# A gate product ahead of v's products, and its weights rounded behind its evacuation, in a two-layer GLA and differential-attention kernel

## The chip, the cores and the metric

One core of a Trainium2 chip runs the whole program. The metric is the device time of one execution in microseconds, the median of several runs. All arithmetic is in fp32 accuracy: TensorE multiplies rounded fp32 values ("high" parts) and adds products with the rounding rest ("low" parts), so nearly every matrix exists as a pair, made by a copy on ScalarE (ACT) and a subtraction on VectorE (DVE).

## The reference, cut to what matters

Sixteen learned rows are put ahead of 512 input rows (528 rows of 1024). Layer one is gated linear attention with four heads, layer two differential attention with eight. What the change touches is the beginning of layer one:

```python
proj = xn @ w_in                       # q, k, v, z and g_lr, of the normalised rows xn
q, k, v, z, g_lr = jnp.split(proj, ...)
lg = jax.nn.log_sigmoid(g_lr @ w_gate_up + b_gate) / GLA_TAU
b = jnp.cumsum(lg, axis=2)             # the decay within a chunk
```

`g_lr` has only 16 columns (the gate product below), `w_gate_up` turns them into 1024 (the decay products). Everything else of a head needs the sums `b`; where they fall too low the program takes another, slower path (the branch below).

## The kernel before, in words

The order of the work. PE's instructions run in the order in which the program issues them. On ACT and DVE a scheduler chooses the order when the program is built, by dependences and priorities (`urgent` raises one), except within a stretch called `ordered` (from L686 to `ordered.close()`, L993), whose ACT and DVE instructions keep the program's order among themselves. `issue_after(i)` puts what a block issues on i's engine behind i. `behind_gate()` (L316) does that with the two instructions in `W.gated`, one of ACT and one of DVE.

Filling. A `Weaver` W holds a queue of generators, each a projection that yields after some matmuls the time that they should take. `W.fill(us)` issues steps of the queue until their times add up to at least `us`. `W.defer(us, f)` calls f once so much has been filled in since. So the program's straight code (the gate product, the decays, the branch) is interleaved on PE with products of v, q, k and z by the numbers in these calls.

Plain products. v (two of its column blocks of 256), q and k of head 0 are made by `plain_unit`: a block of 128 columns takes 8 steps of 0.66, each 6 matmuls of 264 columns, into two PSUM banks; 8 such blocks (4 of v, 2 of q, 2 of k) are 64 steps. The banks alternate (`pb_pair`): `bv`, `by` for v's first block, then two banks `bx` for the second. The gate product's results `pgs` (L955) stand in two `bx` banks, the ones that v's second block takes next. A finished v block is copied out on ACT (L892, behind the gate), and 2.4 us of filled steps later four transposes and one short one turn it to token order (L833, L834, into PSUM tiles `ps`, of which there are four). z's products follow the plain ones; they use sums of token halves (`token_sums(0)` to `token_sums(5)`), whose splits are again one ACT and one DVE instruction of 128x1056.

The gate product (L959 to L983). For each of 8 blocks k of the input width, four matmuls at L967 add to `pgs`; after each but the first stands one step of v's products:

```python
        if k >= 1:                                   # L969
            W.fill(0.6)
...
        if k == 5:                                   # L975
...
            wur = T(gp, [P, D], F32R, "z")           # L981
            act.activation(wur, wup, AF.Copy)
            dve.tensor_tensor(wur[64:96], wup[64:96], wur[64:96].bitcast(F32), op=ALU.subtract)
```

`wur` is the rounded `w_gate_up`, in 128x1024, with rows 64 to 95 turned into the low part (L982 on ACT, L983 on DVE).

Its evacuation (L984 to L992). For each of the two banks: an ACT copy (L987), two DVE copies (L988, L989), an ACT copy (L990) and a DVE subtraction (L991), into `gs` and `gh`. The last ACT and DVE instructions of these become `W.gated`.

The decays (L1015 to L1028). After `W.fill(4.0)`, `decay(k)` for k = 0 to 7: two matmuls of `wur` with `gs` into two `ps` tiles (L1006), three functions on ACT (L1007 to L1009), a DVE subtraction that frees the tiles (L1012) and a running sum on DVE into `b_all` (L1013); then `W.fill(3.5)` (2.0 after the first). After k = 1 to 4 comes `token_sums(k - 1)`, with `behind_gate()` from k = 3.

The branch (L1034 to L1264). DVE reduces `b_all` to a flag `fl` (L1034, L1035). After `W.fill(2.4)` a product of one element brings the flag to partition 0 (L1258), DVE turns it into an integer `fi` (L1259), PE fills in 4.0 more, and every engine reads `fi` and branches. In these inputs the other path is not taken.

Of the kernel before, what the change touches and what calls it, by code (L numbers as in the profile page):

```python
# [11 lines left out]
F32 = mybir.dt.float32  # L12
F32R = mybir.dt.float32r
I32 = mybir.dt.int32
U16 = mybir.dt.uint16
AF = mybir.ActivationFunctionType
ALU = mybir.AluOpType
# [3 lines left out]
P = 128  # L21
D = 1024
# [186 lines left out]
def trunk(ctx, tc, x, meta, g_norm, gla_w_in, gla_w_gate_up, gla_b_gate, gla_gnorm, gla_w_out,  # L209
# [3 lines left out]
    act, dve, pe, pool, sp = nc.scalar, nc.vector, nc.tensor, nc.gpsimd, nc.sync  # L213
# [17 lines left out]
    def T(p, shape, dt, tag, **kw):  # L231
        uid[0] += 1
        return p.tile(shape, dt, tag=tag, name=f"{tag}_{uid[0]}", **kw)
# [10 lines left out]
    def ps_tile():  # L244
        return T(ps_pool, [P, 512], F32, "ps")
# [43 lines left out]
    W = Weaver()  # L289
# [26 lines left out]
    def behind_gate():  # L316
        st = ExitStack()
        for i in W.gated:
            st.enter_context(tc.issue_after(i.ins))
        return st  # L320
# [211 lines left out]
    gp = gctx.enter_context(tc.tile_pool(name="gp", bufs=1))  # L532
# [62 lines left out]
    def warm_up(n, t=None):  # L595
        t = warm if t is None else t
        for _ in range(n):
            pe.matmul(t[:, :P], ones, ones, start=True, stop=True)
# [23 lines left out]
    wup = v2[1][:, 0, :]  # L622
# [43 lines left out]
    def raw_turn(b, halves=range(2)):  # L666
        n = BLK[b][1]
        for i in halves:
            pt = ps_tile().rearrange("p (k c) -> p k c", k=4)
            raws.setdefault(b, []).append(pt)  # L670
            for k in range(4):
                pe.transpose(pt[:, k, :n], xt[b][:n, (4 * i + k) * P:(4 * i + k + 1) * P], ident[:n, :n])

    def raw_copy(b, i, eng):
        t0, n = BLK[b]
        o, pt = hT[:, 4 * i:4 * i + 4, t0:t0 + n], raws[b][i][:, :, :n]
        if eng is act:
            act.activation(o, pt, AF.Copy)
        else:
            dve.tensor_copy(o, pt)  # L680
# [79 lines left out]
    def token_sums(n):  # L760

        if n == 0:
            dve.tensor_tensor(x1, x1, x2, op=ALU.subtract)
        elif n == 1:
            split(*X["t1"], x1)
        elif n == 2:
            dve.tensor_tensor(x2, x4, x2, op=ALU.subtract)
            dve.tensor_tensor(x4, x4, x1, op=ALU.add)
        elif n == 3:
            split(*X["t2"], x4, scale=-1.0)  # L770
        elif n == 4:
            dve.tensor_tensor(x3, x4, x3, op=ALU.subtract)
            split(*X["t4"], x3)
        else:
            X["t3"] = x_parts(6)
            split(*X["t3"], x2)
# [182 lines left out]
    for k in range(KT):  # L959
        for n in range(2):  # L960
            for i, x in enumerate((X["b11"], b12) if k < 4 else (X["b21"], X["b22"])):
                if k == 0:
                    warm_up((3, 3, 1, 4)[2 * n + i], idle)
                if (k, 2 * n + i) in turns_of:
                    b, half = turns_of[k, 2 * n + i]
                    raw_turn(b, [half])
                pe.matmul(pgs[i][:112, :HT], glr[:, k, :], x[n][:, k % 4, :],  # L967
                          start=k == 0 and n == 0, stop=k == KT - 1 and n == 1)
        if k >= 1:  # L969
            W.fill(0.6)  # L970
        if k == 1:
            raw_turn(3, [0])
        if k == 4:
            raw_turn(0)
        if k == 5:  # L975
            for b in (3, 4):
                for i in range(2):
                    raw_copy(b, i, act)
            raw_copy(0, 0, dve)
            raw_copy(0, 1, act)  # L980
            wur = T(gp, [P, D], F32R, "z")  # L981
            act.activation(wur, wup, AF.Copy)  # L982
            dve.tensor_tensor(wur[64:96], wup[64:96], wur[64:96].bitcast(F32), op=ALU.subtract)  # L983
    gh = T(gp, [P, L], F32R, "a0")  # L984
    for i, pg in enumerate(pgs):
        cs = slice(i * HT, (i + 1) * HT)
        act.activation(gs[0:RANK, cs], pg[0:RANK, :HT], AF.Copy)  # L987
        dve.tensor_copy(gs[64:64 + RANK, cs], pg[64:64 + RANK, :HT])  # L988
        dve.tensor_copy(gs[96:96 + RANK, cs], pg[96:96 + RANK, :HT])  # L989
        high = act.activation(gh[32:32 + RANK, cs], pg[32:32 + RANK, :HT], AF.Copy)  # L990
        low = dve.tensor_tensor(gs[32:32 + RANK, cs], pg[32:32 + RANK, :HT], gh[32:32 + RANK, cs].bitcast(F32), op=ALU.subtract)  # L991
    W.gated = (high, low)  # L992
    ordered.close()  # L993
    ws.held = 0
# [6 lines left out]
    @urgent  # L1001
    def decay(k):
        e = tmp()
        pus = [ps_tile()[:, :HT] for _ in range(2)]
        for i, pu in enumerate(pus):
            pe.matmul(pu, wur[:, k * P:(k + 1) * P], gs[:, i * HT:(i + 1) * HT], start=True, stop=True)  # L1006
            act.activation(e[:, i * HT:(i + 1) * HT], pu, AF.Abs)  # L1007
        act.activation(e, e, AF.Exp, scale=-1.0)
        act.activation(e, e, AF.Ln, bias=one1)  # L1009
        for i, pu in enumerate(pus):  # L1010
            ei = e[:, i * HT:(i + 1) * HT]
            dve.scalar_tensor_tensor(ei, pu, 0.0, ei, op0=ALU.min, op1=ALU.subtract)  # L1012
        dve.tensor_tensor_scan(b_all[:, k, :], carry, e, 0.0, op0=ALU.mult, op1=ALU.add)  # L1013
# [5 lines left out]
    for k in range(KT):  # L1019
        decay(k)  # L1020
        if k == KT - 1:

            tc.mark_branch_hint_location("steep", "LikelyTaken", engines=[
                mybir.EngineType.PE, mybir.EngineType.DVE, mybir.EngineType.Activation, mybir.EngineType.SP])
        W.fill(3.5 if k else 2.0)
        if 1 <= k <= 4:
            with behind_gate() if k >= 3 else ExitStack():
                token_sums(k - 1)  # L1028

    eL = T(hp, [P, KT, 5], F32, "eL")  # L1030
# [222 lines left out]
        W.fill(2.0)  # L1253
        rows(4, prev)

    W.fill(2.4)
    pf = ps_tile()
    pe.matmul(pf[0:1, 0:1], fl[:, 1:2], one1, start=True, stop=True)  # L1258
    told = urgent(dve.tensor_copy)(fi, pf[0:1, 0:1])  # L1259
# [600 lines left out]
def build(shapes):  # L1860
    import concourse.bacc as bacc

    nc = bacc.Bacc("TRN2", target_bir_lowering=False, num_devices=1, dynamic_dma_scratch_size=512)
    args = [nc.dram_tensor(f"in_{n}_dram", shp, F32, kind="ExternalInput").ap() for n, shp in shapes]
    args.append(nc.dram_tensor("out_0_dram", (1, NR, D), F32, kind="ExternalOutput").ap())
    with tile.TileContext(nc) as tc:
        trunk(tc, *args)
    return nc
# [15 lines left out]
```

## Time and profile before

| | us |
|---|---|
| median of 3 runs (lowest, highest) | 991.65 (991.6, 993.63) |
| the profiled execution | 992.74 |
| its span | 991.0 |
| busy in it: PE, PE's weight loads | 971.3, 916.7 |
| busy in it: DVE, ACT, POOL | 777.4, 616.1, 50.8 |
| mean granted TensorE clock | 0.995 |

A line of a timeline gives the start, the busy time, engine, line of the source, operation, output and inputs, shape and count of like instructions in a row; in brackets the idle time of the engine before it and what ended that. A line of waits gives the total, the number and the longest. A line of windows gives the stretch, its length, then busy time and instructions of PE, PE's weight loads, DVE, ACT and POOL, the granted clock, the DMA engines' share and GB/s.

### The profile page before, as it was taken

Reading aid. Unit: us, or ns where it says so; the run is one execution under the profiler, and the core shown is the slowest. Engines: PE = TensorE matmul, PEld = TensorE weight load, DVE = VectorE, ACT = ScalarE, POOL = GpSimd, SP = SyncE. Lnnn points to the kernel's source line nnn. Section 1 sums busy time; section 2 is a strip of 40 time slices with the busy share of each in tenths; the row PEclk is TensorE's granted clock in tenths of the full one; section 3 lists DMA queues with packets and bytes.
Section 4 is the critical chain, followed back from the end, with each engine's and each line's share of the span. In section 5 each row is a group of like instructions: output and inputs, shape, how many; then the busy total and the mean of one; then the engine's idle time right before and its main releaser. Section 6 shows DMA issues by size and latency. Waiting matters only on the chain. (4 is left out here: it accounts for less than half of the span.)

```text
span 991.0 us, 18184 instructions
## 1 busy us (share of the span) xinstructions
PE 971.3 (98%) x7065; PEld 916.7 (93%) x7065; DVE 777.4 (78%) x1584; ACT 616.1 (62%) x1306; POOL 50.8 (5%) x68
## 2 busy tenths in 40 slices
PE   8899999999999999999999999999999999999997
PEld 8898999999999999999899899898998999988896
DVE  7779886788778788556998895887967869677785
ACT  7575865475646656536567676466765667655583
POOL 1000000000000100000000101001010010000001
PEclk9899999999999999999999999999999999999999
DMA  8313313632363312222232524335353351523212
GB/s 192 82 48 88 89 44 130 139 94 78 108 155 91 86 44 85 87 85 77 82 105 61 133 85 145 86 97 135 85 146 86 84 145 45 181 56 89 86 64 85
DMA packets 150474, 96.27 MB, mean 97 GB/s; under 512 B 33117, under 2 KB 136829, under 8 KB 150384
## 3 DMA queue, kind: packets, MB, share of 16 engines
q1 hardware_dynamic: 147504, 89.61, 33.1%
q10 hardware_dynamic: 2880, 5.46, 1.6%
q8 instruction: 57, 0.93, 0.4%
q14 instruction: 33, 0.27, 0.1%
HBM read 83.64 MB, written 7.57 MB: 92 GB/s over the span
## 5 line engine op out<-in xcount | busy, mean ns | idle before, releaser
L270 DVE TENSOR_TENSOR wl<-raw,wh 128x1024 fp32r<-128x1024 f32 x98 | 119.6, 1222 | 27.1 <-ACT wh L269 20.2
L269 ACT ACTIVATE wh<-raw 128x1024 fp32r<-128x1024 f32 x98 | 103.0, 1053 | 52.9 <-PE by L938 27.0
L402 PE MATMUL bv<-x,wh 128*128 128x264 f32 (+1 forms) x656 | 97.5, 287 | 0.8 <-DVE t L448 0.6
L402 PE MATMUL bx<-x,wh 128*128 128x264 f32 (+1 forms) x640 | 95.4, 286 | 0.3
L402 PEld LDWEIGHTS bv<-x,wh 128*128 128x128 f32 x656 | 86.2, 189 | 2.0 <-DVE t L448 1.3
L402 PEld LDWEIGHTS bx<-x,wh 128*128 128x128 f32 x640 | 84.6, 188 | 1.6 <-ACT u L423 0.5
L392 PE MATMUL bx<-x,wh 128*128 128x512 f32 (+1 forms) x256 | 62.5, 386 | 0.0
L423 ACT ACTIVATE u<-bx 128x264 f32<-128x264 f32 (+1 forms) x120 | 45.4, 379 | 24.6 <-PE bx L402 22.2
L270 DVE TENSOR_TENSOR wl<-sum,wh 128x1024 fp32r<-128x1024 f32 x41 | 50.1, 1221 | 11.8 <-ACT wh L269 10.5
L1618 ACT ACTIVATE p<-p,st 128x528 f32<-128x528 f32 (+3 forms) x64 | 36.4, 569 | 30.9 <-DVE st L1616 30.5
L402 PE MATMUL bv<-x,wl 128*128 128x264 f32 (+1 forms) x328 | 54.9, 284 | 0.0
L1654 POOL TENSOR_TENSOR st<-st,mhalf 128x1 f32<-128x1 f32 x32 | 30.7, 959 | 466.5 <-ACT on L1652 422.4
L402 PE MATMUL bx<-x,wl 128*128 128x264 f32 (+1 forms) x320 | 53.6, 285 | 0.0
L392 PEld LDWEIGHTS bx<-x,wh 128*128 128x128 f32 x256 | 44.5, 188 | 7.9
L269 ACT ACTIVATE wh<-sum 128x1024 fp32r<-128x1024 f32 x41 | 43.3, 1056 | 12.0 <-PE bv L402 4.7
L402 PE MATMUL by<-x,a12h 128*128 128x264 f32 (+1 forms) x320 | 47.0, 286 | 0.2
L269 ACT ACTIVATE a11h<-raw 128x512 fp32r<-128x512 f32 x41 | 25.7, 627 | 33.4 <-DMA raw<-in_diff_w_in_dram 18.0
L402 PE MATMUL bx<-x,a11h 128*128 128x264 f32 (+1 forms) x320 | 46.3, 285 | 0.0
L402 PEld LDWEIGHTS bv<-x,wl 128*128 128x128 f32 x328 | 45.8, 188 | 0.0
L402 PEld LDWEIGHTS bx<-x,wl 128*128 128x128 f32 x320 | 45.0, 188 | 0.4 <-DVE wl L270 0.2
L402 PEld LDWEIGHTS bx<-x,a11h 128*128 128x128 f32 x320 | 42.2, 188 | 0.8
L402 PEld LDWEIGHTS by<-x,a12h 128*128 128x128 f32 x320 | 41.8, 188 | 0.7 <-DVE t L448 0.4
(479 smaller groups left out, 2647.1 us busy)
## 6 DMA issues: line engine op xcount, KB each, us to landing
raw<-in_gla_w_in_dram SPq DMA_DIRECT2D x48, 512.0 KB, 4.2
raw<-in_diff_w_in_dram SPq DMA_DIRECT2D x42, 512.0 KB, 5.5
raw<-in_diff_w_in_dram SPq DMA_DIRECT2D x11, 1024.0 KB, 5.8
raw<-in_gla_w_out_dram SPq DMA_DIRECT2D x8, 1024.0 KB, 5.9
raw<-in_diff_w_out_dram SPq DMA_DIRECT2D x8, 1024.0 KB
vd<-planes ACTq DMA_DIRECT2D x12, 268.0 KB, 3.0
vd<-keep ACTq DMA_DIRECT2D x8, 264.0 KB, 2.3
T<-bdr SPq DMA_DIRECT2D x8, 264.0 KB, 3.4
```

The source lines that it names most:

```text
L269: act.activation(hi, src, AF.Copy)
L270: dve.tensor_tensor(lo, src, hi.bitcast(F32), op=ALU.subtract)
L392: pe.matmul(bank, a[:, k, :], b[k] if n0 is None else b[k][:, n0 + i * nn:n0 + (i + 1) * nn], start=n == 0 and ks[0] == 0, stop=n == len(t ...
L402: pe.matmul(bank[:, :x[q].shape[2]], w[p][:, k * P:(k + 1) * P], x[q][:, k, :], start=first and i == 0, stop=i == len(PASSES) - 1, skip_gr ...
L423: W.moved = act.activation(t, self.bx[:, :self.n], AF.Copy, scale=self.sc)
L1618: act.activation(p[:, :nk], p[:, :nk], AF.Exp, scale=-1.0, bias=st[:, m:m + 1], accum_out=st[:, 2 + m:3 + m])
L1654: pool.tensor_tensor(ms, ms, mhalf[:, :1], op=ALU.pow)
```

## The change

Three edits go together. The steps of v's products inside the gate product's loop end with k = 4, so three of seven are issued behind it. `wur` is rounded behind the evacuation instead of at k = 5, and `W.gated` now holds these two instructions; with it, `token_sums(1)` is put behind the gate as well. And 5.0 instead of 2.4 is filled in ahead of the branch's product, which takes up what the loop no longer issues.

```diff
-        if k >= 1:
+        if 1 <= k <= 4:
             W.fill(0.6)
...
             raw_copy(0, 0, dve)
             raw_copy(0, 1, act)
-            wur = T(gp, [P, D], F32R, "z")
-            act.activation(wur, wup, AF.Copy)
-            dve.tensor_tensor(wur[64:96], wup[64:96], wur[64:96].bitcast(F32), op=ALU.subtract)
     gh = T(gp, [P, L], F32R, "a0")
     for i, pg in enumerate(pgs):
         cs = slice(i * HT, (i + 1) * HT)
...
         high = act.activation(gh[32:32 + RANK, cs], pg[32:32 + RANK, :HT], AF.Copy)
         low = dve.tensor_tensor(gs[32:32 + RANK, cs], pg[32:32 + RANK, :HT], gh[32:32 + RANK, cs].bitcast(F32), op=ALU.subtract)
+    wur = T(gp, [P, D], F32R, "z")
+    high = act.activation(wur, wup, AF.Copy)
+    low = dve.tensor_tensor(wur[64:96], wup[64:96], wur[64:96].bitcast(F32), op=ALU.subtract)
     W.gated = (high, low)
...
         if 1 <= k <= 4:
-            with behind_gate() if k >= 3 else ExitStack():
+            with behind_gate() if k >= 2 else ExitStack():
                 token_sums(k - 1)
...
-    W.fill(2.4)
+    W.fill(5.0)
     pf = ps_tile()
     pe.matmul(pf[0:1, 0:1], fl[:, 1:2], one1, start=True, stop=True)
```

## The prediction, made before the run

> **What bounds the kernel now.** I read the page first, then the list of waits of PE, then PE's timeline from 14 to 130 us, then those of DVE and ACT over the same stretch, then the windows.
>
> ```profile
> span 991.0 us, 18184 instructions
> PEclk9899999999999999999999999999999999999999
> ```
>
> The profiled execution took 992.74 us: the span and 1.74 around it. The median of the three runs shown is 991.65, 1.09 less; I take differences from the trace and subtract them from the median. PE is the bound nearly everywhere, so a change is worth what it takes from PE's idle or slow time. The granted clock is below nine tenths only in the second of the 40 slices (24.8 to 49.6 us), where the change lies.
>
> ```profile
> PE bx L845 <- DVE a L991: 2.8, 2, 1.4
> PE ps L1258 <- DVE fl L1035: 2.0, 1, 2.0
> ```
>
> These are the two longest entries among PE's waits in the whole span (total, times, longest), and the change touches both. PE's timeline around them:
>
> ```profile
> 25.80 0.74 PE L967 MATMUL bx<-x,kd 128*112 128x264 f32 x4
> 27.11 0.65 PE L967 MATMUL bx<-x,kd 128*112 128x264 f32 x4
> 28.33 0.65 PE L967 MATMUL bx<-x,kd 128*112 128x264 f32 x4
> 31.82 0.39 PE L845 MATMUL bx<-x,wh 128*128 128x264 f32 x1 [1.40 <-DVE a L991]
> 33.61 3.67 PE L845 MATMUL bx<-x,wh 128*128 128x264 f32 x15 [1.40 <-DVE a L991]
> 38.83 1.03 PE L833 MATMUL ps<-ident,t 128*128 128x128 f32 x4
> 39.73 1.70 PE L845 MATMUL bx<-x,wh 128*128 128x264 f32 x12
> 41.27 0.41 PE L1006 MATMUL ps<-a,z 128*128 128x264 f32 x2
> 56.90 0.28 PE L845 MATMUL bv<-x,wh 128*128 128x264 f32 x1
> 74.62 0.40 PE L1006 MATMUL ps<-a,z 128*128 128x264 f32 x2
> 76.33 2.08 PE L845 MATMUL bx<-x,wh 128*128 128x264 f32 x16
> 79.22 2.11 PE L845 MATMUL bx<-x,wh 128*128 128x264 f32 x16
> 84.30 0.19 PE L1258 MATMUL ps<-ones,fl 128*1 128x1 f32 x2 [1.99 <-DVE fl L1035]
> ```
>
> From 76.33 to 79.22 lie 24 matmuls: 0.12 us each, 0.73 for a step of six. The three groups at L967 are the gate product's last (k = 5, 6, 7), each followed by a step of v's products. Then v's second block wants the gate product's two PSUM banks, and waits for their evacuation, bank by bank, from 30.42 (31.82 less 1.40) to 33.61.
>
> ```profile
> 30.43:33.61 3.18, 0.39 (x2) 0.19 (x2) 2.51 (x10) 1.63 (x4) 0.00 (x0) 0.89 0.00 0
> 33.61:39.73 6.12, 6.12 (x28) 6.06 (x29) 3.54 (x3) 1.24 (x3) 0.00 (x0) 0.50 0.00 1
> ```
>
> The first row has 0.39 us of PE in 3.18; in the second the granted clock is 0.50. So the wait is paid twice: 23 matmuls from 33.61 to 38.83 took 5.22 us, where 23 x 0.12 = 2.8 would do, and the five transposes until 39.73 lost half of their 0.90. Together 2.9 us.
>
> Why the evacuation is late stands in DVE's and ACT's timelines:
>
> ```profile
> 27.51 1.26 DVE L270 TENSOR_TENSOR x<-y,x 128x1056 fp32r<-128x1056 f32 x1 [1.02 <-ACT x L269]
> 28.78 1.22 DVE L983 TENSOR_TENSOR z<-v,z 32x1024 fp32r<-32x1024 f32 x1
> 30.01 0.43 DVE L988 CAST a<-bx 16x264 fp32r<-16x264 f32 x1
> 31.34 0.43 DVE L991 TENSOR_TENSOR a<-bx,a 16x264 fp32r<-16x264 f32 x1
> 33.13 0.42 DVE L991 TENSOR_TENSOR a<-bx,a 16x264 fp32r<-16x264 f32 x1 [0.45 <-ACT a L990]
> 27.38 1.04 ACT L982 ACTIVATE z<-v 128x1024 fp32r<-128x1024 f32 x1
> 28.90 0.38 ACT L987 ACTIVATE a<-bx 16x264 fp32r<-16x264 f32 x1 [0.47 <-PE bx L967]
> ```
>
> DVE does the subtraction of token sum 1 (`x<-y,x`, 1.26) and that of the gate weights (`z<-v,z`, 1.22), and only then takes up the evacuation, 1.1 us after ACT had begun it. From there a half takes 1.77 us (30.01 to 31.77; 31.77 to 33.55).
>
> **The change, part by part.**
>
> Steps behind the gate product. Two of the three steps lie between the last gate groups, so the group at 28.33 moves to 26.87 and ACT's first copy from 28.90 to 27.44. Token sum 1 is now held behind the gate and the weights' rounding comes after the evacuation, so both rows ahead of 30.01 leave. The first half then ends at 27.44 + 0.45 + 1.77 = 29.65, the second at 31.4. PE still has the moved steps: four steps (24 matmuls, 2.9 us) behind the last gate group, to 30.4 as now. The first bank is free before that, the second is awaited for 0.9 us instead of 2.8. PE runs on at 31.45 instead of 33.61: 2.15 saved. With 0.9 us idle instead of 3.2 I expect the clock to stay at 1.0: 2.9 more. Sum 5.05.
>
> [...]
>
> Rounding of the gate weights. It is one ACT instruction (1.04) and one DVE (1.22), now on the path of the first decay product (L1006). ACT's last copy of the evacuation ends one subtraction (0.43) before 31.4, so the rounding runs 31.0 to 32.0 and the subtraction to 33.3. The first decay product now stands behind 11 steps instead of 14 (four plus seven): three steps into the second block, at 31.45 + 17 x 0.12 = 33.5. Cost 0 by 0.2 us of margin; with one more 1.26 us instruction ahead of it on DVE PE would stand 1.1 us, and v's products behind it. It can't gain. What W.gated holds (the split of v's next weights, v's evacuation, token sums 1 to 3) queues behind these two instead, from 33.3 on DVE; now it starts there behind 33.55, so nobody waits longer. No DMA is moved; the weight loads follow the splits that free their buffers.
>
> Decays three steps earlier. The steps counted: 64 plain ones in all; now 7 + 7 + 4 + 7 x 6 = 60 and four in the fill of 2.4, so the branch product stands exactly behind the 64th. After: 57, and the fill of 5.0 takes the seven left and two small steps of z's first product (6 matmuls, 0.73). So PE comes to L1258 at 82.31 - 5.05 + 0.73 = 78.0, with 0.73 of later work done. Whether `fl` is ready then is DVE's affair:
>
> ```profile
> 33.55:84.24 50.69, 48.24 (x371) 47.48 (x371) 40.30 (x64) 35.59 (x70) 0.00 (x0) 0.94 0.23 63
> 64.33:84.24 19.91, 17.78 (x145) 17.36 (x143) 19.84 (x36) 13.35 (x23) 0.00 (x0) 1.00 0.20 53
> 40.54 0.69 DVE L270 TENSOR_TENSOR v<-ps,v 128x512 fp32r<-128x512 f32 x1 [3.39 <-ACT v L269]
> 45.20 0.77 DVE L1012 SCALAR_TENSOR_TENSOR t<-ps,t 128x264 f32<-128x264 f32 x2 [0.21 <-ACT t L1009]
> 64.33 0.69 DVE L337 TENSOR_TENSOR sum<-raw 128x512 f32<-128x512 f32 x1 [2.58 <-DMA raw<-in_gla_w_in_dram]
> ```
>
> From the evacuation to `fl` DVE is busy for 40.30 us (third number pair of the row) and idle for 10.39. Lower bound: from 33.3 without any idle time, with token sum 1 added, 33.3 + 40.30 + 1.26 = 74.9. Upper bound: the idle time as now but for the 3.39 that the slow clock made, 81.9. The nearest row between them is the last: from 64.33 DVE never rests until `fl`, and it began then because a load landed, 7.43 us after PE ended v's last block (56.90), which had freed the buffers. With PE 5.05 earlier that is 59.3, and 19.9 on gives 79.2; token sum 1 fits into the idle time before. I take 79.2, the branch product at 79.3, a wait of 1.3 instead of 2.0. Gain so far: 84.30 - 79.3 + 0.73 = 5.7.
>
> A small new wait: the four transposes and the second decay now follow the first decay within 3.4 us, and a decay holds its PSUM tiles for 4.7 (41.27 to 45.97). If the second gets these tiles it waits 1.3, if the transposes' nothing. I count 0.5. No gain is possible there. **Forecast: 5.2 us less, 991.65 - 5.2 = 986.4.**
>
> Behind the branch both PE and DVE start from `fl`, so all shifts alike, and the two rows of waits above are by far the longest: I count nothing as given back.
>
> **The rivals.**
>
> 1. DVE follows at once (the decays come three steps earlier, so one of them fits into the idle 2.58 before the load). Then PE never waits at L1258 and the product runs at 78.0: 7.0 less, 984.6. For it: the row at 64.33. Against it: that DVE is full afterwards.
>
> 2. DVE keeps all its other idle time, `fl` at 81.9: gain 84.30 - 82.0 + 0.73 = 3.0, 988.6.
>
> 3. The clock falls all the same, because 0.9 us and a stall at the first decay lie close together. Then 2.9 goes; with `fl` bound as before 991.65 - 5.2 + 2.9 = 989.3.
>
> 4. Slower: PSUM tiles. Decays release their tiles on DVE (L1012), in an order fixed when the program is built.
>
> ```profile
> 33.59 1.26 DVE L767 TENSOR_TENSOR y<-y,y 128x1056 f32<-128x1056 f32 x1
> 34.76 1.22 DVE L270 TENSOR_TENSOR wl<-raw,wh 128x1024 fp32r<-128x1024 f32 x1
> 35.89 1.25 DVE L768 TENSOR_TENSOR y<-y,y 128x1056 f32<-128x1056 f32 x1
> 42.26 1.26 DVE L273 SCALAR_TENSOR_TENSOR x<-y,x 128x1056 fp32r<-128x1056 f32 x1 [0.66 <-ACT x L272]
> ```
>
> If these four and token sum 1 (6.25 us) all stand ahead of the first L1012, it ends at 33.3 + 6.25 + 0.77 = 40.3. The second decay, at 36.9, waits 3.4, the clock halves (2.9), and the third, whose tiles the second holds, waits as long again: 9.7 lost against 5.05 won. PE is at L1258 at 87.7 and the end moves by 87.7 - 84.30 - 0.73 = 2.7, to 994.3. It decides against the change from a first release behind 40. For it: today's DVE order has all four ahead of 45.20. Against it: the decays are issued as urgent, and L1012 at 45.20 waited for ACT, not for these.
>
> **How the numbers follow.** A measurement of this kernel can tell about 0.2% (2 us) from no change. Forecast, 985.4 to 987.6: 0.43; rival 1: 0.15; rival 2: 0.16; rival 3 or a like loss: 0.11, half of it within 0.2%; rival 4 and slower: 0.15. Faster by over 0.2%: 0.79; same: 0.06; slower: 0.15. The range from 983.8 to 991.2 leaves out rival 4 and a little at either end.
>
> **What would show it.** Right: the last group of L967 at 26.9; L988 within 0.5 us of L987; one wait of L845 of about 0.9 and the clock at 1.0 through 40 us; the first L1006 near 33.6 without a wait on `z`; the branch product between 78 and 80. Wrong: another DVE or ACT instruction of 1 us ahead of L988 or of the gate weights' subtraction, a half clock behind 31 us, L1006 waiting for L1012, or the gain present at the branch product and gone by the end.

## The result, and the profile after

The changed kernel takes 986.66 us (median of four runs, 985.8 to 987.15) against 991.62 before (991.48 to 993.63): 5.0 us less, a ratio of 0.9944 with a 95% interval from 0.9927 to 0.9962. In a later comparison (e12 below) it was 985.59 against 990.67, 5.1 less, 0.9953 (0.9939 to 0.9967). The forecast was 986.4.

The page of the changed kernel:

```profile
span 984.8 us, 18186 instructions
PEclk9999999999999999999999999999999999999999
```

The second slice, at 8 before, is at 9. PE's waits from 14 to 130 us (total, times, longest):

```profile
PE bx L845 <- DVE a L988: 0.9, 1, 0.9
PE ps L1006 <- DVE v L270: 0.2, 1, 0.2
PE bx L402 <- DVE ks L822: 0.2, 1, 0.2
```

The 2.8 at the gate product's banks has become 0.9 (L988 is the line that was L991), the 2.0 at the branch product is gone. PE's timeline, with the rows that answer to those of before:

```profile
26.45 1.71 PE L967 MATMUL bx<-x,kd 128*112 128x264 f32 x12
32.09 2.07 PE L845 MATMUL bx<-x,wh 128*128 128x264 f32 x15 [0.91 <-DVE a L988]
34.24 0.41 PE L1006 MATMUL ps<-a,z 128*128 128x264 f32 x2
38.28 0.73 PE L1006 MATMUL ps<-a,z 128*128 128x264 f32 x2 [0.20 <-DVE v L270]
67.95 0.41 PE L1006 MATMUL ps<-a,z 128*128 128x264 f32 x2
77.68 0.89 PE L402 MATMUL by<-x,a11h 128*128 128x264 f32 x6
78.50 0.19 PE L1258 MATMUL ps<-ones,fl 128*1 128x1 f32 x2
```

The last three gate groups follow one another (26.45, twelve matmuls), the fifteen matmuls behind the wait take 2.07 us instead of 3.67, and the branch product is reached behind the six matmuls of z (77.68) without a wait. DVE's timeline:

```profile
28.49 0.43 DVE L985 CAST a<-bx 16x264 fp32r<-16x264 f32 x1 [1.35 <-ACT a L984]
31.61 0.43 DVE L988 TENSOR_TENSOR a<-bx,a 16x264 fp32r<-16x264 f32 x1 [0.18 <-ACT a L987]
32.69 1.22 DVE L991 TENSOR_TENSOR z<-v,z 32x1024 fp32r<-32x1024 f32 x1 [0.66 <-ACT z L990]
56.03 0.78 DVE L1012 SCALAR_TENSOR_TENSOR t<-ps,t 128x264 f32<-128x264 f32 x2 [0.71 <-ACT t L1009]
60.17 0.69 DVE L270 TENSOR_TENSOR a11l<-raw,a11h 128x512 fp32r<-128x512 f32 x1 [1.12 <-ACT a11h L269]
76.82 0.14 DVE L1035 TENSOR_SCALAR fl<-fl 128x1 f32<-128x1 f32 x1
```

DVE is idle when the gate product ends and takes up the evacuation at once; the weights' subtraction (32.69) comes behind it, and `fl` is ready at 76.96, 1.5 us before PE asks for it.

All these times are some 0.77 late, because this execution lost time at its beginning: the clock fell there. The windows of PE (busy time, granted clock, DMA share, GB/s), first of this execution, then of another of the same kernel (e12):

```profile
8.00:12.00 4.00, 3.39 (x15) 0.58 1.13 297
32.00:36.00 4.00, 3.91 (x32) 1.00 0.01 2
```

```profile
8.00:12.00 4.00, 3.48 (x30) 1.00 1.13 295
```

PE's timeline in that execution of e12:

```profile
25.69 1.71 PE L967 MATMUL bx<-x,kd 128*112 128x264 f32 x12
31.32 2.09 PE L845 MATMUL bx<-x,wh 128*128 128x264 f32 x15 [0.91 <-DVE a L988]
33.49 0.40 PE L1006 MATMUL ps<-a,z 128*128 128x264 f32 x2
77.74 0.19 PE L1258 MATMUL ps<-ones,fl 128*1 128x1 f32 x2
```

The second has the clock at 1.00 from 8 to 12 us, as the profile of before has, so its times are the ones to hold against before: PE runs on at 31.32 instead of 33.61, the first decay is at 33.49 instead of 41.27, and the branch product at 77.74 instead of 84.30.

### The profile page after: what moved, and what is told of

It is laid out like the page before. It is cut to its first block, busy times and chain, and to the rows that moved or that the text cites. A ratio compares the mean times of both kernels' runs of the same rounds, so it can differ in the third digit from the quotient of the medians.

```text
span 984.8 us, 18186 instructions
## 1 busy us (share of the span) xinstructions
PE 969.7 (98%) x7065; PEld 915.2 (93%) x7065; DVE 777.3 (79%) x1584; ACT 615.6 (63%) x1306; POOL 50.7 (5%) x68
## 3 DMA queue, kind: packets, MB, share of 16 engines
q1 hardware_dynamic: 147504, 89.61, 33.5%
## 5 line engine op out<-in xcount | busy, mean ns | idle before, releaser
L270 DVE TENSOR_TENSOR wl<-raw,wh 128x1024 fp32r<-128x1024 f32 x98 | 119.6, 1222 | 26.9 <-ACT wh L269 19.9
L270 DVE TENSOR_TENSOR wl<-sum,wh 128x1024 fp32r<-128x1024 f32 x41 | 50.1, 1221 | 11.0 <-ACT wh L269 9.7
```

Source lines behind the costliest of these rows:

```text
L270: dve.tensor_tensor(lo, src, hi.bitcast(F32), op=ALU.subtract)
```

## The experiments

The theory to be tested: DVE's two instructions of 1.2 us made the evacuation late, the moved steps cover what is left of it, the clock is paid beside the wait, and the branch product waited for the decays' place in the order. Each result stands against the kernel before on the same chip, median against median, with the ratio and its 95% interval. The 59 executions of the kernel before in these comparisons, on three chips, ran from 988.83 to 995.05.

**e1, the steps and the fill alone.**

```diff
-        if k >= 1:
+        if 1 <= k <= 4:
             W.fill(0.6)
...
-    W.fill(2.4)
+    W.fill(5.0)
```

> Before with the three steps behind the gate product and the fill of 5.0, but the weights still rounded at k = 5 and token sum 1 not held back. Theory (DVE is what makes the evacuation late): DVE still does token sum 1 and the weights' subtraction until about 30.0, the evacuation ends near 33.5 as before, v's second block still waits about 2.8 us and the clock still falls to 0.5; only the wait of 2.0 at the branch product goes, because it stands behind more work and the decays are three steps earlier. Time 989 to 990. Rival (the moved steps are what covers the evacuation): the wait at L845 falls to about 1 and the clock stays at 1.0; 986.5 to 987.5.

989.63 against 991.79, 0.9980 (0.9969 to 0.9991). PE's rows:

```profile
33.33 2.72 PE L845 MATMUL bx<-x,wh 128*128 128x264 f32 x15 [1.40 <-DVE a L991]
81.07 0.19 PE L1258 MATMUL ps<-ones,fl 128*1 128x1 f32 x2
```

As the theory had it: the last gate group came 1.5 us earlier and nothing came of it, since DVE started the evacuation at 29.73 behind the same two instructions; PE waited the same 2.8 us, and the clock fell again (0.58 from 34 to 37 us, 0.85 from 37 to 40). The gain of 2.2 lies at the branch product, which waits no longer: `fl` is ready at 79.32.

**e2, the rounding and the gate alone.** The edits to `wur`, `W.gated` and `behind_gate` without the two others.

> Before with the weights rounded behind the evacuation and token sum 1 behind the gate, but the steps and the fill of 2.4 as before. Theory: the last gate group stays at 28.3, ACT's first copy at 28.9, DVE's first at 29.3 instead of 30.0; the evacuation ends 0.7 us earlier, near 32.85, and PE, out of steps at 30.4, waits about 2.1 instead of 2.8. Whether the clock then falls is open: if it does, 990.9, if not, about 988 less what the branch product's wait gives back. The wait at the branch product stays near 2. Rival (all of the gain is in DVE's order): 987.

989.89 against 991.79, 0.9974 (0.9964 to 0.9985). PE's waits:

```profile
PE bx L845 <- DVE a L988: 2.1, 2, 1.4
PE ps L1258 <- DVE fl L1035: 2.0, 1, 2.0
```

Both waits as expected. Whether the clock falls was the open point, and the executions differ in it: those with a mean granted clock of 0.999 took 987.78 to 988.67, those with 0.995 to 0.996 990.49 to 991.34. The two halves of the change, e1 and e2, bring 2.2 and 1.9, together 4.1 of the 5.0; whether the rest is theirs together or scatter can't be told from these runs.

**e3, fill alone.**

```diff
-    W.fill(2.4)
+    W.fill(4.6)
...
         token_sums(4)
-    W.fill(4.0)
+    W.fill(2.0)
```

> Before with 4.6 instead of 2.4 filled in ahead of the branch product and 2.0 instead of 4.0 behind it, so the branch stands behind the same work: six small steps (2.2 us of PE) move from behind the branch product to ahead of it. Theory: the wait of 2.0 at L1258 goes almost wholly and nothing takes its place: 989.6, and no change at the gate product. Rival (DVE is the bound there, so the wait moves to the next product that needs DVE): 991.6.

993.42 against 991.79, 1.0015 (1.0004 to 1.0025): slower. The theory falls for this edit by itself. The wait moved one step ahead:

```profile
84.17 1.00 PE L402 MATMUL bx<-x,a12h 128*128 128x264 f32 x6 [2.05 <-DVE ks L822]
85.10 0.19 PE L1258 MATMUL ps<-ones,fl 128*1 128x1 f32 x2
```

z's second product needs a bank that DVE frees (L822), and DVE is as late with that as with `fl`. Here the added fill hung on the same engine, and nothing was won. Why it is 1.6 slower rather than equal is settled in part only: in its profile the clock falls a second time, behind this wait (0.50 from 86 to 88 us), and over all executions its mean granted clock is 0.9955 against 0.9961 for before on that chip, some 0.6 us of a span. The rest is open.

**e4, the clock at the gate product.** Idle products of ones in PE's wait, six `warm_up` ahead of the first bank and seven ahead of the second:

```diff
                     for bank, x in zip(banks, xs):
+                        if spare is not None and j == n == 0:
+                            warm_up(6 if bank is banks[0] else 7, spare)
                         pe.matmul(bank[:, :HT], ...
```

> Before with 13 idle products of ones (each two 128-column matmuls, 0.22 us) put into PE's wait at L845, six ahead of the first bank and seven ahead of the second, into a spare PSUM tile; they change no result. They take nothing from the wait itself. Theory: the granted clock stays at 1.0 through 40 us, the 23 matmuls behind the wait take 2.8 instead of 5.2 us and the first decay product stands near 38.4 instead of 41.3; how much of the 2.9 reaches the end depends on the branch product, whose wait may grow: 988.7 to 990.5. Rival (the low clock in the record is no cost of its own): first decay product at 41.3, 991.6.

991.30 against 991.79, 0.9992 (0.9980 to 1.0004): no difference that can be told, less than I expected and near what the rival gave, though the rival's reason does not hold. At the gate product the idle products did what they should (the window of PE, its weight loads, DVE, ACT and POOL, then the clock, the DMA share and GB/s):

```profile
33.61:36.53 2.92, 2.92 (x26) 2.91 (x24) 2.92 (x3) 1.26 (x3) 0.00 (x0) 1.00 0.01 3
```

The 28 instructions that took 6.12 us at half clock before, up to 39.73, took 3.4 here, up to 36.99, and the first decay stood at 38.53. But PE still met the branch product's wait, and there the clock fell in this execution (PE's timeline, then its windows):

```profile
81.50 0.19 PE L1261 MATMUL ps<-ones,fl 128*1 128x1 f32 x2 [2.00 <-DVE fl L1038]
```

```profile
82.00:84.00 2.00, 2.00 (x12) 0.53 0.00 0
86.00:88.00 2.00, 2.00 (x18) 1.00 0.51 122
```

(The lines of this kernel stand three further down from there on.) The branch product ran 2.8 us earlier than before (84.30), but by the first product of q and k behind the branch, at 92.26 where before has 92.19, all of that was gone: some 1.7 went to the slow clock (0.53 from 82 to 84 us, 0.62 from 84 to 86), and 1.2 to a pause for which the profile shows no cause:

```profile
91.89 0.53 PE L402 MATMUL by<-x,wl 128*128 128x264 f32 x3 [1.16 <-issue]
```

So in this execution the clock was paid at the second wait instead of the first, and e11 covers both.

**e11, the clock at both waits.** e4 and `warm_up(9, ps_tile())` ahead of the branch product.

> Before with idle products of ones in both of PE's waits: 13 at L845 and nine (2.0 us) ahead of the branch product; they change no result and shorten no wait of the products behind them. Theory: with PE busy in both waits the granted clock stays at 1.0 from 12 us on in every execution; what is left of the spread is the start. Mean granted clock 0.998 to 0.999 instead of 0.996, 989.6 to 990, some 1.7 of the 5 us. Rival (the clock time lost is made up elsewhere, as after e4): 991.5.

989.21 against 990.67, 0.9986 (0.9977 to 0.9995), and all its executions lie between 988.47 and 990.02, where before has 988.83 to 992.86 on the same chip. The mean granted clock is 0.9985 instead of 0.9970. PE's windows over both places:

```profile
34.00:38.00 4.00, 4.00 (x36) 1.00 0.00 0
80.00:84.00 4.00, 4.00 (x35) 1.00 0.00 0
```

The idle products shorten no wait, and 1.5 of the 5 us are there: this much is the clock alone.

**e5, the changed kernel with the fill of 2.4.**

> The changed kernel with 2.4 instead of 5.0 filled in ahead of the branch product, the third edit alone undone. Theory (the flag is ready at 77.0 in the changed kernel, PE comes to its product at 78.5): PE comes 2.9 us earlier, near 75.6, and waits 1.4 us for `fl`; the three plain steps follow behind it. Time 1.2 to 2 us above the changed kernel: 988 to 988.6, more in executions in which that wait brings the clock down. Rival (the earlier decays alone removed the wait, the fill is worth nothing): no wait at L1258, 986.7.

986.83 against 991.49, 0.9956 (0.9942 to 0.9969). The wait is there as expected:

```profile
76.05 0.19 PE L1258 MATMUL ps<-ones,fl 128*1 128x1 f32 x2 [1.19 <-DVE fl L1035]
```

but the time is not the 988 to 988.6 that I expected. Its ratio to before is that of the changed kernel itself (0.9953 in e12), as the rival said for another reason: the 1.2 us do not reach the end. At the first output product (L1206, a head's first result behind the branch) it is at 106.96 where e12 is at 105.82, 1.1 behind; at the last L1206 it is at 398.17 against 397.89. The third edit is worth nothing that can be told here.

**e6, token sum 1 not held behind the gate** (`behind_gate() if k >= 3` in the changed kernel).

> The changed kernel with token sum 1 not held behind the gate (behind_gate from k = 3 as before). Theory: its ACT and DVE instructions slip in ahead of the evacuation again, DVE's first copy of it starts 0.4 to 0.9 us later (behind token sum 1's subtraction instead of at 28.5), the wait at L845 grows from 0.9 to between 1.3 and 1.8, and the clock falls in some executions: 987 to 988.5. Rival (the rounding alone was in the way): the wait stays at 0.9, 986.7.

987.12 against 991.49, 0.9951 (0.9938 to 0.9965). DVE's rows, PE's, and PE's window:

```profile
27.36 1.26 DVE L270 TENSOR_TENSOR x<-y,x 128x1056 fp32r<-128x1056 f32 x1 [1.02 <-ACT x L269]
28.64 0.43 DVE L985 CAST a<-bx 16x264 fp32r<-16x264 f32 x1
```

```profile
32.23 3.42 PE L845 MATMUL bx<-x,wh 128*128 128x264 f32 x15 [1.40 <-DVE a L988]
```

```profile
34.00:36.00 2.00, 2.00 (x11) 0.51 0.00 0
```

The mechanism is as expected: DVE begins 0.9 later (27.71 in e5 without the late start), PE waits 1.6 (0.18 and 1.40), and in this execution the clock fell; two of the five have a mean granted clock of 0.996. In the time it is 0.3 above e5 on the same chip, within the intervals.

**e10, the rounding back at k = 5** (the other edits kept).

> The changed kernel with the gate weights rounded at k = 5 again and the gate at the evacuation's last instructions; the moved steps, the gate for token sum 1 and the fill stay. Theory: without token sum 1 ahead of it the rounding starts on ACT at about 26.2 and its subtraction on DVE at 27.2 to 28.4, so DVE's first copy comes at 28.4 instead of 27.7 (without the late start of the profiled execution), the wait at L845 is 1.6 instead of 0.9, and the clock falls in some executions: 987 to 988. Rival (moving the rounding was needed for the whole gain at the gate): wait 2.8, 989.6.

985.53 against 990.67, 0.9951 (0.9937 to 0.9964), beside 985.59 for the changed kernel itself (e12): no difference. DVE's row, then PE's:

```profile
28.24 0.43 DVE L988 CAST a<-bx 16x264 fp32r<-16x264 f32 x1
```

```profile
31.83 2.07 PE L845 MATMUL bx<-x,wh 128*128 128x264 f32 x15 [1.40 <-DVE a L991]
77.86 0.19 PE L1258 MATMUL ps<-ones,fl 128*1 128x1 f32 x2
```

The wait is 1.4 instead of 0.9 (I expected 1.6), but the clock held in all five executions (0.998 and 0.999), and the time is 1.5 us below the least that I expected. Most of the half microsecond is made up by the second decay, which waits no longer (37.67 against 37.51 in e12), and the branch product is at 77.86 against 77.74. So neither of DVE's two instructions alone had to leave; with both ahead of the evacuation (e1) the wait stayed at 2.8, with one it is 1.4 to 1.6.

**e7, the evacuation operation by operation.** In the changed kernel:

```diff
-    for i, pg in enumerate(pgs):
-        ... the five instructions of one bank, then of the other
+    for pg, cs in halves:
+        act.activation(gs[0:RANK, cs], pg[0:RANK, :HT], AF.Copy)
+    for pg, cs in halves:
+        dve.tensor_copy(gs[64:64 + RANK, cs], pg[64:64 + RANK, :HT])
+        dve.tensor_copy(gs[96:96 + RANK, cs], pg[96:96 + RANK, :HT])
+    for pg, cs in halves:
+        act.activation(gh[32:32 + RANK, cs], pg[32:32 + RANK, :HT], AF.Copy)
+    for pg, cs in halves:
+        dve.tensor_tensor(gs[32:32 + RANK, cs], pg[32:32 + RANK, :HT], gh[32:32 + RANK, cs].bitcast(F32), op=ALU.subtract)
```

> The changed kernel with the gate product's evacuation issued operation by operation instead of bank by bank: ACT's first copies of both banks, then DVE's four, ACT's second copies, DVE's two subtractions. Theory: the chain of ACT and DVE turns inside one bank (1.77 us for three DVE and one ACT instruction) no longer stands twice in a row; DVE's six instructions of 0.43 follow one another, the first bank is free about 1.1 us later than now but still when PE comes, the second 0.9 earlier; the wait at L845 falls from 0.9 to 0 to 0.3, the first decay moves with it. 985.9, a version faster than both. Rival (the weights' rounding or the first decay takes the place of the wait): L1006 waits for it, 986.7.

984.92 against 991.49, 0.9930 (0.9917 to 0.9944): the wait is 0.3, as expected, and the time 1.0 lower than expected.

**e8, one step more behind the gate product.** `1 <= k <= 3`, and `W.fill(4.7)` ahead of the decays.

> The changed kernel with one step more behind the gate product (steps for k = 1 to 3) and 4.7 instead of 4.0 filled in ahead of the first decay, which keeps it at its place in the second block. Theory: the last gate group and the evacuation come 0.7 us earlier, PE has one step more of cover, the wait at L845 falls from 0.9 to about 0.2: 986.0. Rival (ACT's copies of the turned rows or DVE's splits hold the gate product or the evacuation at its present time): the wait stays, 986.7.

985.06 against 991.49, 0.9938 (0.9924 to 0.9951): the wait is 0.2, as expected, and the time 0.9 lower than expected. Both stand some 1.8 below e5 on the same chip, with intervals that touch. The changed kernel itself was not run on that chip.

**e9, both.**

> The changed kernel with both: the evacuation operation by operation, and one step more behind the gate product with 4.7 ahead of the first decay. Theory: each alone left a wait of 0.3 and 0.2 at L845, so together the wait is gone, but there is no more than that to win: 984.5 to 985, no measurable step below either alone. Rival (the two add): 983.5.

984.92 against 990.67, 0.9945 (0.9931 to 0.9958), 0.7 below the changed kernel on that chip, and not to be told from it by the intervals. The wait at L845 is gone and another has come:

```profile
36.89 0.73 PE L1009 MATMUL ps<-a,z 128*128 128x264 f32 x2 [0.65 <-DVE t L1015]
```

The second decay (L1009 here) waits for the first's PSUM tiles, the place that the prediction's slower rival named, at a price of 0.65. It can't be told from e7 and e8 either, which have ratios of 0.9930 and 0.9938 on their chip, so nothing was won by doing both.

**e12, the changed kernel again.**

> The changed kernel once more, beside the others on the same chip, as the measure for e9 and e10: 986.7, mean granted clock about 0.998, a spread of no more than 2 us.

985.59 (985.29 to 986.69), 5.1 below the 990.67 of that chip and 1.1 below what I expected; before is 1.0 lower on that chip too than in the first comparison.

## Why the prediction was right, and where it was not

The gate product: right to 0.15 us. PE was to run on at 31.45 and did at 31.32 (e12), with a wait of 0.9; the weights' subtraction was to end at 33.3 and the first decay to stand at 33.5, and it stood at 33.49 without a wait on `z`. That DVE and not the place of the steps held the evacuation is shown by e1; that the steps and the moves of DVE's work are both needed, by e1 and e2. Of the two moves of DVE's work each alone brings the wait from 2.8 to 1.4 or 1.6 (e6, e10), both bring it to 0.9, and in the time the second can't be told.

The clock: right that it stays at 1.0 there, too high in price. The 2.9 us is what one execution lost, and its clock was lower (0.995) than most. Over the 59 executions of before the mean granted clock is 0.9963, which is 3.6 us of a span; the nine of the changed kernel have 0.9986 (1.4). The difference is 2.2, and e11 alone shows 1.5.

The branch product: the term that failed. I put it at 79.3 with a wait of 1.3; it came at 77.74 without one, as rival 1 had it (78.0). The step was "from 64.33 DVE never rests until `fl`", 19.9 us taken over as they stood. In the changed kernel the stretch from DVE's first work on the load (60.17) to `fl` (76.96) is 16.8, 3.1 less. (In e12 it is 59.26 to 76.06, so the start was forecast right, at 59.3.) DVE's order is not the same as before. First three rows of before, then two of the changed kernel:

```profile
64.94 0.77 DVE L1012 SCALAR_TENSOR_TENSOR t<-ps,t 128x264 f32<-128x264 f32 x2
82.77 0.67 DVE L337 TENSOR_TENSOR sum<-sum,raw 128x512 f32<-128x512 f32 x1
83.48 0.69 DVE L337 TENSOR_TENSOR raw<-raw 128x512 f32<-128x512 f32 x1
```

```profile
76.93 0.69 DVE L337 TENSOR_TENSOR sum<-sum,raw 128x512 f32<-128x512 f32 x1
77.54 0.68 DVE L337 TENSOR_TENSOR raw<-raw 128x512 f32<-128x512 f32 x1
```

The decay whose subtraction stood at 64.94, behind the load, now stands at 56.03, ahead of it; with its running sum that is about 1.9 us. Two sums of weights (L337) stood ahead of `fl` (84.08) and now stand behind it (76.82); that is about 1.2. Rival 1 had named the first; the second nobody had. The new order comes with the moved steps: e1 and e5 have it (in e1 the decay at 58.61 stands ahead of the load at 63.74, and the two sums stand behind `fl`), e2, where the decays keep their place, has that of before.

The new wait at the second decay: 0.2 instead of 0.5, for the copy of the four transposes (L270).

"Nothing is given back": true of some executions and not of others. What PE had won (with the 0.73 of later work at the branch product) was 7.3 us at the branch product, 6.9 at the first output product (112.75 less 105.82) and 6.2 at the end of the span (991.0 less 984.8) in e12; but 6.5, 6.0 and 6.2 in the first profile of the changed kernel, and 7.2, 7.1 and 7.3 in e10. So one execution gave back 1.1, the others 0.3 and nothing. In e12 about half of it lies in one wait of PE, at L1239 for ACT's L1217 (242.70): 1.36 there, 0.85 in before and 0.35 in the first profile, so it varies with the execution. That is also where e5 makes up most of its wait of 1.2 on e12: of the 0.9 that it wins back between the first and the last L1206, 0.6 lies at that place, where it waited 0.72. The rest is open.

And the profiled execution of before, 992.74, lies 1.1 above its own median, which the forecast did not allow for when it took differences from the trace and subtracted them from the median. So 6.2 by the two profiles are 5.0 by the medians. That the forecast of 5.2 comes so near is in part luck: 1.6 too little at the branch product and the 0.5 taken off for a wait that cost 0.2 stand against the 1.1 by which the profile of before was slow (some 0.7 of it the price of the clock, the 2.9 of that execution less the 2.2) and the 1.1 given back in e12.

The rivals: 1 was right about the branch product (78.0) but not about the end, 984.6. 2 and 4 did not happen. Of the five instructions that 4 feared ahead of the first L1012 three stood there in e12, and it ended at 38.1, not at 40.3; the second decay's wait for PSUM tiles turned up at 0.2, and at 0.65 behind L1012 itself in e9. 3 did not happen in any of the nine executions (clock 0.997 or more), though e6 shows how near it is: with 1.6 of waiting the clock fell (0.51 from 34 to 36 us).

## What to carry to other kernels

When an engine whose order the program fixes, as PE here, waits for an evacuation, look first at what the evacuating engine does in that moment: moving cover there (e1) was worth nothing at the gate product, where the wait stayed at 2.8 us, until one of two unrelated instructions had left DVE's queue (1.4 in e10, 1.6 in e6). More fill ahead of a wait won nothing where the filled-in work hung on the same late engine (e3, 993.42 against 991.79), while issuing the decays three steps earlier brought `fl` forward by 4.9 us in e1, where PE itself ran 1.3 earlier (at L834, 38.42 against 39.68). Where executions of a kernel scatter by 6 us, as the 59 of before do (988.83 to 995.05), put each one's granted clock beside its time before you explain anything by one trace.

## What the runs showed of the hardware

Most of the scatter of the kernel before goes with the granted clock that the profiles give for TensorE. Over its 59 executions, with the lost clock time as (1 - mean granted clock) x span, the time is 988.0 + 0.99 x lost (correlation 0.86): 989.1 on average at 0.999, 991.0 at 0.997, 993.3 at 0.995. The same program loses the clock in different places: the first profile of the changed kernel had it at 0.58 from 8 to 12 us, e12 at 1.00. Of the kernels with other edits, e4 lost it behind a single wait of 2.0 us (0.53 from 82 to 84 us), e6 behind waits of 0.18 and 1.40 with one matmul between (0.64 from 32 to 34 us, 0.51 from 34 to 36), while e10 kept it at 1.00 from 32 to 40 us through a wait of 1.40. The length of a wait alone does not decide it in these profiles: behind the branch product's wait of 2.0 it was at 1.00 from 84 to 88 us in before and e2. From 8 to 12 us it was at 0.58 and 0.57 in two profiles, the first of the changed kernel and e7; the longest wait for `y` (L684) was 0.84 and 0.8 there, and before had one of 0.84 as well, up to 8.34, at a clock of 1.00. (The two also waited for a load of `x`, 0.54 and 0.3; before did not.) Behind the 0.9 at L845 it stayed at 1.00 in all three profiles that have that wait (the two of the changed kernel, and e5).
